# A hybrid transformer block in float32r parts: weight parts and FFN inner tiles at varied byte offsets of SBUF

## The chip, the core and the metric

The kernel runs on one core of a Trainium2 chip. The metric is the time of one execution on the device in microseconds; the median of three runs before the change is 2668.3 us (2667.89 to 2669.66).

## The reference

One sequence of 512 tokens with 1024 features passes a first block and then two equal layers of a second block. All is float32.

```python
def first_block(x, p, ...):                     # once
    z = rms_norm(x, norm1_g) @ w_in             # 1024 -> 2304 columns
    mix = concat(gmlp(z), rglru(z), hgrn2(z), pool(z))
    x = x + mix @ w_out
    hf = causal_dwconv(rms_norm(x, norm2_g) @ w_up, ...)   # 1024 -> 2 x 2816
    gt, val = split(hf)
    x = x + (gelu(gt) * val) @ w_down           # 2816 -> 1024
    gate = sigmoid(rms_norm(x, norm3_g) @ w_pg)
    x = x + (p @ w_pe) * gate
    return rms_norm(x, final_g)

def hybrid_layer(x, ...):                       # twice
    proj = (rms(x) * norm1_g) @ w_in            # 1024 -> 7680
    mixed = g0 * (attention @ w_attn_o) + g1 * (rwkv @ w_rwkv_o) + g2 * (retention @ w_ret_o)
    x = x + mixed @ w_out
    h2 = rms(x) * norm2_g
    return x + (silu(h2 @ w_ffn_gate) * (h2 @ w_ffn_up)) @ w_ffn_down
```

## The kernel before

Activations lie transposed: 128 features on the partitions, 512 tokens along a row, so the model's 1024 features are 8 tiles (k tiles) of 128x512 float32, and the 2816 inner features of an FFN are 22.

**Dense products.** Every product with a weight goes through `mac` (lines 135 to 137). Weight and activation are each split into two float32r parts, high and low, and a product takes three passes: high weight on high activation (line 135), high weight on low activation (line 136), low weight on high activation (line 137). Each pass is a matmul of a 128x128 weight (loaded into the array) on a moving tile of 128x512. An M tile of 128 outputs with 8 k tiles is thus 24 matmuls that add up in one PSUM bank.

**Weights** come in chunks of 8 k tiles (128x1024 float32; 7 k tiles in two of three chunks of the FFNs' second product). `chunk` (line 117) takes a raw chunk that SyncE's queue has loaded (`wraw`, three buffers), lets ScalarE round it into `whi` (line 125) and VectorE subtract that from the raw values into `wlo` (line 126). `whi` and `wlo` have two buffers each, used in turn.

**Activations** are split by `split` (line 172) with the same two engines: `x0h` to `x7l` are the parts of the normed input of a projection, `h0h` to `h21l` the parts of the FFN's inner tiles, `mx` those of the gated sum of the branches, `o` those of attention and retention, `BK` those of the RWKV output (its tiles take the place of keys that are no longer needed), and `t` those of the small input p.

**The FFNs.** `ffn1` (line 655) runs 44 M tiles of w_up on x with a convolution behind each, keeps the 22 products as h tiles, and then runs 8 M tiles of w_down on the 22 h tiles. `ffn2` (line 1342) does the same with gate and up in each of the two layers. In the mixers, dense tiles that nothing waits for are put between the steps of the mixer (`pump`).

**Order.** Instructions are issued in an order that a scheduler makes from the program, and tiles are placed in SBUF by pools in the order in which they are asked for. As built, a row of a partition starts at these bytes, modulo 256:

| tiles | 128x512 matmuls they move in | offset of the moving tile | offset of the weights |
|---|---|---|---|
| x | 6864 | 32 | 32 |
| h | 1584 | 160 | 32 |
| o | 384 | 160 | 32 |
| mx | 384 | 160 | 32 |
| BK | 192 | 0 | 32 |
| t | 48 | 0, 64 or 192 | 32 |

A k tile's weights are 512 bytes of a row, and tiles are 2048 or 4096 bytes long, so the offset is the same for all tiles of a kind, for both buffers and for high and low parts.

Of the kernel before, what the change touches and what calls it, by code (L numbers as in the profile page):

```python
# [11 lines left out]
F32R = mybir.dt.float32r  # L12
# [8 lines left out]
P = 128  # L21
# [13 lines left out]
class Kern:  # L35
    def __init__(self, tc, io, taps=None):
        self.tc, self.nc, self.io = tc, tc.nc, io
        self.taps = taps or {}
        self.n = 0
        self.fill, self.credit = deque(), 0.0  # L40
        self.early = deque()
        self.sx = ""
        self.pa, self.pr, self.pp, self.pi, self.pc, self.pt, self.pl, self.px = 7.0, 4.0, 2.0, 1.7, 2.5, 6.0, 6.0, 5.2

    # Dense tiles that nothing waits for yet are kept in a queue; the mixers let
    # some of them in between their own steps, so that the tensor engine has work.
# [70 lines left out]
    def chunk(self, src):  # L117
        """One chunk of a weight: its float32 values, and their two parts."""
        nc = self.nc
        n = src.shape[-1]  # L120
        raw = self.early.popleft() if self.early else self.fetch(src)
        hi = self.tile(self.wp, [P, 1024], "whi", F32R)
        lo = self.tile(self.wp, [P, 1024], "wlo", F32R)
        with self.tc.high_priority(offset=300):
            nc.scalar.copy(hi[:, :n], raw[:, :n])  # L125
            nc.vector.tensor_tensor(lo[:, :n], raw[:, :n], hi[:, :n].bitcast(F32), ALU.subtract)  # L126
        return hi, lo

    def mac(self, ps, w, xs, first, last):
        """ps += w.T @ x over the k tiles in xs, in three passes."""  # L130
        hi, lo = w
        n = len(xs)
        for k, (xh, xl) in enumerate(xs):
            c = slice(k * P, (k + 1) * P)
            self.nc.tensor.matmul(ps, hi[:, c], xh, start=first and k == 0, stop=False)  # L135
            self.nc.tensor.matmul(ps, hi[:, c], xl, start=False, stop=False)  # L136
            self.nc.tensor.matmul(ps, lo[:, c], xh, start=False, stop=last and k == n - 1)  # L137

    def dense(self, wname, m, xs, kcuts=None):
        """M tile m of a weight applied to the k tiles xs (pairs of parts)."""  # L140
        src = self.io[wname]
        ps = self.tile(self.mm, [P, 512], "mm")
        kcuts = kcuts or [len(xs)]
        k0 = 0
        for i, kn in enumerate(kcuts):
            w = self.chunk(src[m, :, k0 * P:(k0 + kn) * P])
            self.mac(ps, w, xs[k0:k0 + kn], i == 0, i == len(kcuts) - 1)
            k0 += kn
        return ps

    def dense2(self, wname, xs, use):
        """A weight with 4 k tiles: two M tiles to a chunk; use(m, psum)."""
        src = self.io[wname]
        for j in range(src.shape[0]):
            hi, lo = self.chunk(src[j])
            for i in range(2):
                ps = self.tile(self.mm, [P, 512], "mm")
                o = slice(i * 512, (i + 1) * 512)
                self.mac(ps, (hi[:, o], lo[:, o]), xs, True, True)
                use(2 * j + i, ps)  # L160

    def split_into(self, hi, lo, src, scale=1.0):
        """Two float32r parts of src * scale: hi + lo is exact."""
        nc = self.nc
        nc.scalar.activation(hi, src, AF.Copy, scale=scale)  # L165
        if isinstance(scale, float) and scale == 1.0:
            nc.vector.tensor_tensor(lo, src, hi.bitcast(F32), ALU.subtract)
        else:
            nc.vector.scalar_tensor_tensor(lo, src, scale, hi.bitcast(F32), ALU.mult, ALU.subtract)  # L169
        return hi, lo  # L170
# [6 lines left out]
    def rsqrt(self, v, n):  # L177
        """v ** -0.5 for a small [128, n] tile of positive values."""
        nc = self.nc
        y = self.small("rsq", n)  # L180
        t = self.small("rst", n)
        yi = y.bitcast(I32)
        nc.vector.tensor_scalar(yi, v.bitcast(I32), 1, None, ALU.logical_shift_right)
        nc.vector.tensor_scalar(yi, yi, -1.0, float(0x5F3759DF), ALU.mult, ALU.add)
        for _ in range(3):
            nc.vector.tensor_tensor(t, y, y, ALU.mult)
            nc.vector.scalar_tensor_tensor(t, t, -0.5, v, ALU.mult, ALU.mult)
            nc.vector.scalar_tensor_tensor(y, t, 1.5, y, ALU.add, ALU.mult)
        return y

    def bcast(self, col):
        """[128 tokens, 4] -> PSUM [128, 512]: each token's value down a column."""
        ps = self.psum()
        for b in range(NW):
            self.nc.tensor.transpose(ps[:, b * P:(b + 1) * P], col[:, b:b + 1].to_broadcast([P, P]), self.ident)  # L195
        return ps

    def bcast_heads(self, col):
        """[128 tokens, 4 blocks x 2 heads] -> PSUM [2 x 64 features, 512 tokens]."""
# [7 lines left out]
    def token_sum(self, acc, ps, col):  # L207
        """Sum over features of acc into column col + 4 b of ps."""
        for b in range(NW):
            self.nc.tensor.matmul(ps[:, col + b:col + b + 1], acc[:, b * P:(b + 1) * P], self.ones,  # L210
                                  start=True, stop=True)
# [13 lines left out]
    def norm_scale(self, acc):  # L225
        """The broadcast 1 / rms of the tokens, as an SBUF tile."""
# [32 lines left out]
    def mixers1(self, c2, x, xg, rb, pe):  # L259
# [19 lines left out]
        # small parameters  # L279
# [16 lines left out]
        # columns, the longest mixer's first  # L296
# [30 lines left out]
        # p @ w_pe, halved for the gate that comes later  # L327
# [29 lines left out]
        # the order of the k tiles on the host: d, a, b, c  # L357
# [50 lines left out]
    def rglru_consts(self, tp):  # L408
        nc, V = self.nc, self.vec
        # 2 softplus(-lam): e = exp(-|lam|), log1p(e) by the series of atanh  # L410
# [18 lines left out]
        # softplus(-lam) = max(-lam, 0) + 2 acc;  sp = twice that  # L429
# [73 lines left out]
    def hgrn2(self, zq, zf, zig, lvm, tp, yp):  # L503
        nc, V = self.nc, self.vec
        # lower bound: a softmax over the one layer, less its own first row
# [24 lines left out]
        # masked scores [s, t], one level of block size after another  # L530
        # (heads of one parity, a pair of windows: one PSUM bank)
# [57 lines left out]
        # values and decayed keys by token  # L589
# [10 lines left out]
        # states at the starts of the windows, block diagonal over pairs of heads  # L600
# [39 lines left out]
    def head_rms(self, dst, src, nh, tp, xi=None, xi2=None):  # L640
        """dst = src / rms over the last axis of [128, nh, 64] (src in PSUM); of src * xi, where given."""
# [13 lines left out]
    def ffn1(self, x, acc, xg, pe, xs_p):  # L655
        tc, nc, io, V = self.tc, self.nc, self.io, self.vec
        rb = self.norm_scale(acc)
        with tc.tile_pool(name="f1h", bufs=1) as hp, tc.tile_pool(name="f1t", bufs=2) as fp:
            hid = []
            for j in range(FT):  # L660
# [14 lines left out]
                hid.append(self.split(hp, r[1], f"h{j}"))  # L675
# [8 lines left out]
        # the gate, and the two norms that follow it  # L684
# [3 lines left out]
        with tc.tile_pool(name="f1g", bufs=2) as gp:  # L688
# [14 lines left out]
            # y = a / rms(x4) with a = x4 * final_g; with v and w the means of the squares of  # L703
            # x4 and a, the norm of y on top comes to a * (w + EPS * (v + EPS)) ** -0.5
# [42 lines left out]
    def rwkv(self, c):  # L747
# [21 lines left out]
        # halves of parameters that go with tanh  # L769
# [33 lines left out]
        for p in range(4):  # L803
# [3 lines left out]
            # decays  # L807
# [13 lines left out]
            # in-context rate  # L821
# [4 lines left out]
            # keys  # L826
# [13 lines left out]
            # b, scaled; the order of the two halves of a chunk turns with its parity  # L840
# [8 lines left out]
            # bonus  # L849
# [6 lines left out]
            # values by token  # L856
# [6 lines left out]
            # scores  # L863
# [10 lines left out]
            # keys as they stand at the end of the chunk  # L874
# [6 lines left out]
    def rwkv_inverse(self, SC, kp):  # L881
        """The transposed inverses of I - A (64 x 64) in place of the A of SC."""
# [24 lines left out]
        # rows of the first diagonal block, for the block below it  # L907
# [28 lines left out]
    def rwkv_chain(self, SC, AR, BK, UV, end, gd, g2, kp):  # L936
# [29 lines left out]
        def ahead(c):  # L966
            """What a chunk needs apart from the state: decayed keys by token, products with the values."""
# [97 lines left out]
    def evac(self, dst, ps, scale=1.0):  # L1065
        """dst = ps * the tokens' 1 / rms (* scale)."""
# [42 lines left out]
    def att_proj(self, ap):  # L1109
# [10 lines left out]
        # keys and values  # L1120
# [17 lines left out]
        # queries: tile g has head g (of the first key head) over head 4 + g  # L1138
# [66 lines left out]
    def ret_proj(self, rp, rt):  # L1205
        """Queues the columns of the retention, and what is done to them one by one."""
# [48 lines left out]
    def retention(self, rp, op, q, k, vt, sg, cn):  # L1255
        nc, l = self.nc, self.l
        # the queries, keys and values, where the queue still has any
# [61 lines left out]
    def combine(self, oa, oc, mp):  # L1319
        """The gated sum of the three branches (twice it, halved in the split)."""  # L1320
# [21 lines left out]
    def ffn2(self, xd, acc, xg, out):  # L1342
        tc, nc, io, V, l = self.tc, self.nc, self.io, self.vec, self.l
        rb = self.norm_scale(acc)
        with tc.tile_pool(name="f2h", bufs=1) as hp, tc.tile_pool(name="f2t", bufs=2) as fp:
            hid = []
            for j in range(FT):
# [7 lines left out]
                hid.append(self.split(hp, g, f"h{j}"))  # L1355
# [21 lines left out]
def _w(a, per=1, cols=None, rows=None):  # L1377
    """[K, M] -> chunks [M tiles / per, 128, per * K tiles * 128], contiguous for a partition."""
# [13 lines left out]
def _col(v):  # L1392
    """[n * 128] -> [128, n]"""
# [3 lines left out]
def _constants():  # L1397
# [19 lines left out]
    # rotary angles and decays of the retention  # L1417
# [101 lines left out]
```

## Time and profile before

| | |
|---|---|
| median of 3 runs | 2668.3 us |
| span of the profiled execution, first to last instruction | 2666.0 us |
| TensorE matmul busy | 2579.1 us, 97%, 13104 records |
| TensorE weight load busy (beside matmuls) | 2052.8 us, 77% |
| VectorE busy | 1491.5 us, 56% |
| ScalarE busy | 893.7 us, 34% |
| GpSimd busy | 378.5 us, 14% |
| mean granted TensorE clock | 0.985 |

The profile gives for each instruction a start, a duration, its line and its tiles; matmuls are pipelined, so the duration of one reaches beyond the start of the next, and the distance between starts tells how fast they follow each other. [...]

### The profile page before, as it was taken

How to read it: one execution, taken by the hardware profiler on the slowest of the kernel's cores; microseconds unless marked ns; L12 is line 12 of the kernel's file. 1: busy time of each engine (PE TensorE's matmuls, PEld its weight loads, DVE VectorE, ACT ScalarE, POOL GpSimd, SP SyncE). 2: the span in 40 equal slices, each digit the busy share in tenths (PEclk: the TensorE clock that was granted, in tenths of full speed). 3: DMA queues.
4: the chain of work that ended last, by engine and by line, in shares of the span. 5: the costliest groups of instructions: out<-in, count | busy, mean ns of one | idle time of the engine just before them, and what ended most of it. 6: DMA issues, size and time to landing. Idle time of an engine off the chain costs nothing. (4 is left out here: it accounts for less than half of the span.)

```text
span 2666.0 us, 33302 instructions
## 1 busy us (share of the span) xinstructions
PE 2579.1 (97%) x13104; PEld 2052.8 (77%) x13104; DVE 1491.5 (56%) x2546; ACT 893.7 (34%) x1342; POOL 378.5 (14%) x277
## 2 busy tenths in 40 slices
PE   8989999999998999999999999998999999999999
PEld 6767888887776877677788887767877677788887
DVE  8775666336788455565443333788455565444322
ACT  4343444225332333522322222322333423332221
POOL 2111111013120001005311101120000004211100
PEclk9999999999999999999999999999999999999999
DMA  4132223334223143226422334223152226422332
GB/s 148 64 103 85 98 95 95 93 104 139 87 91 107 60 154 95 70 87 206 137 95 97 99 123 127 83 80 107 43 174 88 79 72 213 143 95 95 99 114 96
DMA packets 99502, 282.51 MB, mean 106 GB/s; under 512 B 13201, under 2 KB 14225, under 8 KB 99217
## 3 DMA queue, kind: packets, MB, share of 16 engines
q1 hardware_dynamic: 97616, 277.52, 31.8%
q10 hardware_dynamic: 1728, 2.87, 0.3%
q8 instruction: 103, 1.69, 0.3%
q14 instruction: 55, 0.44, 0.1%
HBM read 244.42 MB, written 31.72 MB: 104 GB/s over the span
## 5 line engine op out<-in xcount | busy, mean ns | idle before, releaser
L125 ACT CAST whi<-wraw 128x1024 fp32r<-128x1024 f32 (+1 forms) x400 | 414.6, 1037 | 1110.1 <-PE mm L136 735.1
L126 DVE TENSOR_TENSOR wlo<-wraw,whi 128x1024 fp32r<-128x1024 f32 (+1 forms) x400 | 491.9, 1230 | 246.6 <-ACT whi L125 237.1
L1352 POOL TENSOR_TENSOR fg<-fg,rb 128x512 f32<-128x512 f32 x44 | 78.3, 1780 | 396.1 <-ACT fg L1351 396.1
L135 PE MATMUL mm<-x0h,whi 128*128 128x512 f32 x286 | 116.2, 407 | 8.1 <-ACT x0h L165 8.1
L220 POOL TENSOR_TENSOR acc<-acc,sq 128x512 f32<-128x512 f32 x49 | 77.8, 1587 | 325.9 <-ACT sq L219 325.9
L137 PE MATMUL mm<-x0h,wlo 128*128 128x512 f32 x286 | 114.1, 399 | 6.0 <-DVE wlo L126 5.7
L135 PE MATMUL mm<-x2h,whi 128*128 128x512 f32 x286 | 114.3, 400 | 2.2 <-ACT x2h L165 2.2
L136 PE MATMUL mm<-x0l,whi 128*128 128x512 f32 x286 | 113.7, 397 | 1.2 <-DVE x0l L169 1.2
L136 PE MATMUL mm<-x2l,whi 128*128 128x512 f32 x286 | 114.6, 401 | 0.0
L136 PE MATMUL mm<-x5l,whi 128*128 128x512 f32 x286 | 112.9, 395 | 1.6 <-DVE x5l L169 1.6
L135 PE MATMUL mm<-x3h,whi 128*128 128x512 f32 x286 | 113.9, 398 | 0.0
L137 PE MATMUL mm<-x1h,wlo 128*128 128x512 f32 x286 | 113.7, 398 | 0.0
L136 PE MATMUL mm<-x3l,whi 128*128 128x512 f32 x286 | 113.1, 395 | 0.7 <-DVE x3l L169 0.7
L137 PE MATMUL mm<-x2h,wlo 128*128 128x512 f32 x286 | 113.7, 398 | 0.0
L136 PE MATMUL mm<-x1l,whi 128*128 128x512 f32 x286 | 113.3, 396 | 0.3 <-DVE x1l L169 0.3
L1354 DVE TENSOR_TENSOR fg<-fg,mm 128x512 f32<-128x512 f32 x44 | 30.3, 688 | 148.8 <-PE mm L137 148.8
L135 PE MATMUL mm<-x5h,whi 128*128 128x512 f32 x286 | 113.4, 397 | 0.0
L137 PE MATMUL mm<-x6h,wlo 128*128 128x512 f32 x286 | 113.3, 396 | 0.0
L135 PE MATMUL mm<-x6h,whi 128*128 128x512 f32 x286 | 113.3, 396 | 0.0
L135 PE MATMUL mm<-x7h,whi 128*128 128x512 f32 x286 | 113.2, 396 | 0.0
L137 PE MATMUL mm<-x7h,wlo 128*128 128x512 f32 x286 | 113.1, 396 | 0.0
L135 PE MATMUL mm<-x1h,whi 128*128 128x512 f32 x286 | 113.1, 395 | 0.0
(757 smaller groups left out, 6132.5 us busy)
## 6 DMA issues: line engine op xcount, KB each, us to landing
wraw<-in_w_in_dram SPq DMA_DIRECT2D x138, 512.0 KB, 3.5
wraw<-in_w_ffn_dram SPq DMA_DIRECT2D x88, 512.0 KB, 3.4
wraw<-in_w_up_dram SPq DMA_DIRECT2D x44, 512.0 KB, 3.3
wraw<-in_w_ffn_down_dram SPq DMA_DIRECT2D x32, 448.0 KB, 3.4
wraw<-in_w_out_dram SPq DMA_DIRECT2D x24, 512.0 KB, 3.5
gates<-gt SPq DMA_DIRECT2D x48, 256.0 KB, 2.1
cg<-gates SPq DMA_DIRECT2D x32, 256.0 KB, 3.8
gt<-xres SPq DMA_DIRECT2D x32, 256.0 KB, 3.3
```

The costliest lines, as they stand in the source:

```text
L125: nc.scalar.copy(hi[:, :n], raw[:, :n])
L126: nc.vector.tensor_tensor(lo[:, :n], raw[:, :n], hi[:, :n].bitcast(F32), ALU.subtract)
L135: self.nc.tensor.matmul(ps, hi[:, c], xh, start=first and k == 0, stop=False)
L136: self.nc.tensor.matmul(ps, hi[:, c], xl, start=False, stop=False)
L137: self.nc.tensor.matmul(ps, lo[:, c], xh, start=False, stop=last and k == n - 1)
L220: (eng or nc.gpsimd).tensor_tensor(acc, acc, s, ALU.add)
L1352: nc.gpsimd.tensor_tensor(g, g, rb, ALU.mult)
L1354: nc.vector.tensor_tensor(g, g, ps, ALU.mult)
```

## The change

No instruction is added, removed or moved: on each of the five engines the instructions, their order and their waits are the same. What changes is where two kinds of tiles start in SBUF.

```diff
     def chunk(self, src):
         raw = self.early.popleft() if self.early else self.fetch(src)
-        hi = self.tile(self.wp, [P, 1024], "whi", F32R)
-        lo = self.tile(self.wp, [P, 1024], "wlo", F32R)
+        o = 8 * (self.nw % 4)
+        self.nw += 1
+        hi = self.tile(self.wp, [P, 1056], "whi", F32R)[:, o:o + 1024]
+        lo = self.tile(self.wp, [P, 1056], "wlo", F32R)[:, o:o + 1024]
...
+    def split_at(self, pool, src, tag, o):
+
+        hi, lo = (self.tile(pool, [P, T + 8], tag + c, F32R)[:, o:o + T] for c in "hl")
+        return self.split_into(hi, lo, src)
...
     # ffn1
-                hid.append(self.split(hp, r[1], f"h{j}"))
+                hid.append(self.split_at(hp, r[1], f"h{j}", 0))
...
     # ffn2
-                hid.append(self.split(hp, g, f"h{j}"))
+                hid.append(self.split_at(hp, g, f"h{j}", 2 + 2 * l))
```

The rest of the diff takes out comments. The tiles of `whi` and `wlo` are 128 bytes longer, so the two buffers start 128 apart modulo 256, and a chunk's parts start another 0, 32, 64 or 96 bytes in, by the chunk's number modulo 4. The h tiles are 32 bytes longer, so each next one (h0h, h0l, h1h, ...) starts 32 bytes further on modulo 256; in the two layers of the second block they start another 8 and 16 bytes in. As built:

| tiles | offset before | offset after |
|---|---|---|
| whi, wlo | 32 | 32, 192, 96, 0, chunk by chunk |
| h in ffn1 | 160 | 160, 192, 224, 0, 32, 64, 96, 128 in turn |
| h in ffn2 of the first layer | 160 | the same and 8 |
| h in ffn2 of the second layer | 160 | the same and 16 |
| x, o, mx, BK, t | as above | unchanged |

## Rows read from the trace of the kernel before

**Rows 1.** The page: span, and busy time with share and count.
```profile
span 2666.0 us, 33302 instructions
PE 2579.1 (97%) x13104; PEld 2052.8 (77%) x13104; DVE 1491.5 (56%) x2546; ACT 893.7 (34%) x1342; POOL 378.5 (14%) x277
```
**Rows 2.** Stretch, length; busy us (count) of PE, PEld, DVE, ACT, POOL; clock; DMA.
```profile
250.00:460.00 210.00, 210.00 (x929) 173.87 (x927) 140.56 (x212) 93.30 (x117) 25.14 (x20) 1.00 0.29 97
480.00:580.00 100.00, 100.00 (x431) 80.41 (x430) 31.09 (x33) 26.54 (x32) 7.76 (x5) 1.00 0.31 92
640.00:950.00 310.00, 284.81 (x1950) 224.48 (x1949) 225.94 (x426) 105.97 (x161) 40.85 (x32) 0.96 0.27 92
```
**Rows 3.** Timeline of TensorE, w_up of ffn1: start us, duration us, operation.
```profile
399.70 0.39 PE L135 MATMUL mm<-x3h,whi 128*128 128x512 f32 x1
...
401.97 0.39 PE L136 MATMUL mm<-x6l,whi 128*128 128x512 f32 x1
```
**Rows 4.** Timeline of TensorE, w_up at a granted clock of 0.50, and that clock.
```profile
234.81 0.63 PE L136 MATMUL mm<-x4l,whi 128*128 128x512 f32 x1
...
238.23 0.63 PE L135 MATMUL mm<-x7h,whi 128*128 128x512 f32 x1
...
235.00:239.00 4.00, 4.00 (x11) 0.50 0.00 0
```
**Rows 5.** Timeline of TensorE, w_down of ffn1.
```profile
474.06 0.39 PE L136 MATMUL mm<-h0l,whi 128*128 128x512 f32 x1
474.28 0.40 PE L137 MATMUL mm<-h0h,wlo 128*128 128x512 f32 x1
474.75 0.40 PE L136 MATMUL mm<-h1l,whi 128*128 128x512 f32 x1
...
476.39 0.39 PE L137 MATMUL mm<-h3h,wlo 128*128 128x512 f32 x1
```
**Rows 6.** Timeline of TensorE, output projection of the first layer.
```profile
1265.69 0.40 PE L136 MATMUL mm<-mx4l,whi 128*128 128x512 f32 x1
...
1268.94 0.40 PE L135 MATMUL mm<-mx1h,whi 128*128 128x512 f32 x1
```
**Rows 7.** Timeline of TensorE, RWKV output projection of the first layer.
```profile
951.10 0.40 PE L135 MATMUL mm<-BK,whi 128*128 128x512 f32 x1
...
952.97 0.40 PE L136 MATMUL mm<-BK,whi 128*128 128x512 f32 x1
```
**Rows 8.** Timeline of TensorE, projection tiles after a break in attention.
```profile
1089.10 0.40 PE L137 MATMUL mm<-x5h,wlo 128*128 128x512 f32 x1
...
1091.41 0.39 PE L135 MATMUL mm<-x1h,whi 128*128 128x512 f32 x1
```
**Rows 9.** Groups by line of TensorE: count, busy us, mean ns, idle before.
```profile
L135 PE MATMUL mm<-x3h,whi 128*128 128x512 f32 x286 | 113.9, 398 | 0.0
L135 PE MATMUL mm<-h0h,whi 128*128 128x512 f32 x24 | 9.5, 398 | 0.0
L136 PE MATMUL mm<-o,whi 128*128 128x512 f32 x128 | 50.5, 394 | 0.0
L136 PE MATMUL mm<-BK,whi 128*128 128x512 f32 x64 | 25.5, 399 | 0.0
L135 PE MATMUL mm<-mx2h,whi 128*128 128x512 f32 x16 | 6.3, 395 | 0.0
L135 PE MATMUL mm<-t,whi 128*128 128x512 f32 x16 | 6.5, 405 | 0.0
```
**Rows 10.** Groups by line of VectorE: count, busy us, mean ns, idle before.
```profile
L671 DVE SCALAR_TENSOR_TENSOR fc<-fe,pv,fc 128x512 f32<-128x512 f32 x88 | 65.9, 749 | 2.5 <-ACT fc L669 0.9
L1350 DVE TENSOR_TENSOR fg<-mm,rb 128x512 f32<-128x512 f32 x44 | 30.4, 692 | 114.0 <-PE mm L137 113.8
L667 DVE TENSOR_TENSOR fe<-mm,rb 128x512 f32<-128x512 f32 x44 | 30.3, 688 | 24.2 <-PE mm L137 24.2
L850 DVE SCALAR_TENSOR_TENSOR t<-t,pv,t 128x512 f32<-128x512 f32 x8 | 5.9, 740 | 0.0
```

More of the change, by code (lines that the diff above doesn't have):

```diff
@@ L39, in __init__ @@
         self.n = 0
+        self.nw = 0
         self.fill, self.credit = deque(), 0.0
```

## The prediction

> **What bounds the kernel now.** I read the busy shares first: TensorE is busy 2579.1 of the 2666.0 us of the span, 97%, and no other engine comes near it [rows 1]. So I asked next where it does not stand still at all. In the rows by stretch it is busy for the whole of 250 to 460 us (tiles of w_up, moving tiles x) and of 480 to 580 us (tiles of w_down, moving tiles h), at a granted clock of 1.00; in the mixers, 640 to 950 us, it is busy 284.81 of 310 us [rows 2]. In an FFN the time is thus a number of matmuls times the distance from one start to the next, and that distance is the only thing that moving data in SBUF can change. The order and the waits of all five engines are the same in both programs.
>
> The distance is read from starts in the timeline. Moving tiles x, at byte 32 of 256 as the weights are: ten starts from 399.70 to 401.97, 0.227 us each [rows 3]. [...] Moving tiles h, at byte 160 with weights at 32: ten starts from 474.06 to 476.39, 0.233 us each, alternately 0.22 to 0.23 and 0.23 to 0.24 [rows 5]. Tiles mx, also 160 against 32: 14 starts in 3.25 us, 0.2321 [rows 6]. Tiles BK, 0 against 32: eight in 1.87 us, 0.2338 [rows 7]. Same shape, same engine, same clock: what differs is where the moving tile lies. After a break x needs some ten starts to come back to its pace: 2.31 us for ten from 1089.10 on, 0.231 each [rows 8].
>
> So of the three pairs of offsets that can be seen for long, two run at 0.232 to 0.234, and one, equal offsets, at 0.2267, the value I use for it: it lies between the 0.227 of the starts and the 0.226 of the 929 matmuls in 210 us, those cut at the ends counted [rows 2].
>
> **The change part by part.** The counts: 24 groups of 286 matmuls on x (6864), 66 groups of 24 on h (1584), and 3 times 128 on o, 3 times 64 on BK, 24 times 16 on mx, 48 on t (1008) [rows 9]. 3168 of the 6864 are in the three FFNs (44 M tiles of 24 matmuls each, three times); 3696 are in projections.
>
> 1. *Weights at 32, 192, 96 and 0 in turn, x still at 32.* A quarter of the chunks keeps the equal pair, three quarters get pairs that the trace does not show. Bounds for such a pair: 0.2267, if it settles as the equal pair does, and 0.2338, the slowest seen. One of three pairs seen settles, so I take two of the new ones at 0.233 and one at the value of a pair that settles. A chunk has 24 matmuls and now differs from the chunk ahead, so even a pair that settles must first find its pace: ten at 0.231 and 14 at 0.2267 are 0.2285 on the average. The three new pairs then give (2 x 0.233 + 0.2285)/3 = 0.2315, and with the quarter at 0.2285 the mean is 0.2308. In the FFNs: 3168 x (0.2308 - 0.2267) = +13.0 us, with nothing beside it, since TensorE never stops there. In the projections there are breaks already, so I start from 0.2275: 3696 x 0.0033 = +12 us. Of this part the mixers hide some, where TensorE waits for others for 25 of 310 us [rows 2]; but what waits there waits for VectorE and ScalarE chains that in their turn wait for matmuls behind the dense tiles, so I count three quarters, +9 us.
>
> 2. *h tiles 32 bytes further apart, and 0, 8 or 16 bytes on by FFN.* The moving offset now changes from one matmul to the next and runs through eight values against four of the weights; 1584 matmuls. No settled pattern can form. Bounds 0.2267 and 0.2338 again; I take 0.232, between the 0.231 of unsettled x and the 0.233 of h today: 1584 x -0.0013 = -2 us.
>
> 3. *o, mx, BK, t against the varied weights.* 1008 matmuls at 0.232 to 0.234 today, and I leave them there: 0, and at the bounds -6 or +1 us.
>
> 4. *ScalarE and VectorE read and write the same tiles at odd offsets.* The trace has this already: the multiply that writes 8 bytes into its tile takes 688 ns, the one that writes from the tile's start 692; the multiply-add that reads 4 and 8 bytes in takes 749, one that reads from the start 740 [rows 10]. 0 us; even 9 ns on each of the 800 splits of weights would lie on engines that are busy 56% and 34% of the span [rows 1].
>
> 5. *More SBUF* (512 bytes a partition for weights, 32 a tile of h): no instruction and no wait changes. 0.
>
> [...]
>
> Sum: 13.0 + 9 - 2 = +20 us. The profiled execution has a span of 2666.0 us and the median of the runs is 2668.3, so 2.3 us lie around the span: 2666.0 + 20 + 2.3 = 2688 us.
>
> **The rivals.**
>
> *Nothing settles (slower still).* Each chunk breaks the pace and no new pair settles: x runs at 0.2325 throughout. 3168 x 0.0058 + 3696 x 0.005 x 0.75 - 2 = 18.4 + 13.9 - 2 = +30, 2698 us; at 0.2338 for all x it would be +40. For it: two of three pairs seen. Against it: the equal pair stays in a quarter of the chunks.
>
> *Only the moving tile's own offset counts (no change).* x stays at 32 and at 0.2267 whatever the weights do; h takes a mean over eight offsets, say 0.230: 1584 x -0.0033 = -5, 2663 us, and about 2668 if h stays. For it: in the trace the weights never move, so the two causes cannot be told apart. [...]
>
> *Spreading works (faster).* Weights and moving data that start in different places stay out of each other's way; x keeps 0.2267 and h, mx, o and BK come down to it: -1584 x 0.0066 - 1008 x 0.006 = -16.5, 2652 us. It decides if unequal offsets cost less than equal ones. [...] Against it: the only equal pair in the trace is the fastest one. [...]
>
> **How the numbers follow.** Forecast (one or two of the new pairs settle) 0.42; nothing settles 0.23; only the moving tile counts 0.18; spreading works 0.17. The likeliest gives 2688 us. Its own range is 2678 (all three new pairs settle within their chunk, +10) to 2696. The range to hold the time 8 times in 10 leaves out most of the gain below and the slowest pace for all x above: 2658 to 2703. What a measurement of this kernel can tell from no change is about 0.2%, 5.3 us. Slower: the first two cases nearly whole, 0.64. No change: most of the third and the edges of the first, 0.16. Faster: the fourth and the end of the third where h gains its 5 us, 0.20.
>
> **What would show it.** In the profile after, starts in the w_up stretch should be 0.227 us apart in at most a quarter of the chunks and 0.23 or more in the others, and 1000 matmuls there should take some 231 us instead of 227. In w_down the even alternation should be gone and the mean be near 0.232. Durations on ScalarE and VectorE should stay. The forecast is wrong if x stays at 0.227 in chunks of all four weight offsets (third case), if any chunk runs steadily below 0.2267 (fourth), or if the mixers take the slower tiles without getting longer.

## The result, and the profile after

| | us | runs |
|---|---|---|
| before, median | 2668.1 | 4 (2667.68 to 2669.66) |
| after, median | 2686.44 | 4 (2681.3 to 2686.72) |
| after / before | 1.0065 | 95% interval 1.005 to 1.0079 |
| span of the profiled execution, before | 2666.0 | |
| span of the profiled execution, after | 2684.9 | |

The changed kernel is slower by 18.3 us, 0.65%. The forecast was 2688 us. The page of the changed kernel (span, then busy time, share of the span and count of each engine) shows where it lies:

```profile
span 2684.9 us, 33302 instructions
PE 2602.1 (97%) x13104; PEld 2052.2 (76%) x13104; DVE 1490.5 (56%) x2546; ACT 894.0 (33%) x1342; POOL 378.7 (14%) x277
```

Against [rows 1], matmul busy time has grown by 23.0 us with the same 13104 matmuls, while VectorE, ScalarE and GpSimd differ by at most 1 us: all of it is on TensorE. The windows of the changed kernel in w_up and w_down (stretch, length, busy us and count of PE, PEld, DVE, ACT, POOL, clock, DMA share, GB/s) answer to the first two of [rows 2]:

```profile
250.00:460.00 210.00, 210.00 (x907) 170.06 (x907) 137.47 (x208) 90.17 (x115) 24.56 (x19) 1.00 0.30 96
480.00:590.00 110.00, 110.00 (x476) 89.05 (x475) 36.00 (x39) 30.75 (x37) 9.03 (x6) 1.00 0.33 97
```

In w_up the same 210 us, at the same clock and without a gap, hold 907 matmuls in place of 929. In w_down 476 fit into 110 us, 0.231 each, and before 431 into 100, 0.232 each: no loss there. In the mixers the same stretch of time no longer holds the same work; they are read further down, between equal places of the program.

Where x lost is plain from the first matmul of each chunk of 24. The timeline of TensorE in the changed kernel (start us, duration us, operation), w_up of ffn1, five chunks, whose weights lie at byte 32, 192, 96, 0 and 32 again:

```profile
304.12 0.39 PE L138 MATMUL mm<-x0h,whi 128*128 128x512 f32 x1
...
309.57 0.39 PE L138 MATMUL mm<-x0h,whi 128*128 128x512 f32 x1
...
315.17 0.39 PE L138 MATMUL mm<-x0h,whi 128*128 128x512 f32 x1
...
320.77 0.40 PE L138 MATMUL mm<-x0h,whi 128*128 128x512 f32 x1
...
326.37 0.39 PE L138 MATMUL mm<-x0h,whi 128*128 128x512 f32 x1
```

The chunk at 32, where x lies too, takes 5.45 us, 0.2271 a matmul; the other three take 5.60 us each, 0.2333. Duration says nothing of this, 0.39 or 0.40 us throughout: only the starts do. Over the whole trace, at full clock and without breaks, the distance between starts of x within a chunk is 0.2276 with weights at 32, 0.2335 at 192, 0.2332 at 96 and 0.2332 at 0.

In w_down the order of one slow and one less slow start [rows 5] is gone. TensorE's timeline of the changed kernel, the first nine products of w_down:

```profile
482.10 0.40 PE L138 MATMUL mm<-h0h,whi 128*128 128x512 f32 x1
482.33 0.40 PE L139 MATMUL mm<-h0l,whi 128*128 128x512 f32 x1
482.56 0.39 PE L140 MATMUL mm<-h0h,wlo 128*128 128x512 f32 x1
482.80 0.39 PE L138 MATMUL mm<-h1h,whi 128*128 128x512 f32 x1
...
484.18 0.39 PE L138 MATMUL mm<-h3h,whi 128*128 128x512 f32 x1
```

Nine in 2.08 us are 0.231; the mean over all h is 0.2322, before 0.2333.

A budget of the whole program follows from the first matmul of each stretch. The timelines give these starts for ffn1 and the stretch behind it, first of before:

```profile
227.04 0.39 PE L135 MATMUL mm<-x0h,whi 128*128 128x512 f32 x1
...
473.82 0.40 PE L135 MATMUL mm<-h0h,whi 128*128 128x512 f32 x1
...
597.02 0.39 PE L135 MATMUL mm<-x0h,whi 128*128 128x512 f32 x1
```

and of after:

```profile
230.15 0.39 PE L138 MATMUL mm<-x0h,whi 128*128 128x512 f32 x1
...
482.10 0.40 PE L138 MATMUL mm<-h0h,whi 128*128 128x512 f32 x1
...
604.58 0.39 PE L138 MATMUL mm<-x0h,whi 128*128 128x512 f32 x1
```

w_up went from 473.82 - 227.04 = 246.78 to 251.95 us (+5.2), w_down from 123.20 to 122.48 (-0.7), and the next 350 us, with gate, projections and the RWKV mixer up to its output at 948.29 and 955.18, from 351.27 to 350.60 (-0.7). Read so throughout, from the first matmul to the last:

| stretch | after minus before, us |
|---|---|
| projections and mixers of the first block | +3.0 |
| w_up; gate and up of the two layers | +5.2, +6.6, +5.3 |
| w_down; down of the two layers | -0.7, -0.1, -0.9 |
| last gate and projections up to the RWKV output, twice | -0.7, -0.7 |
| RWKV output to attention output, twice | +1.0, +1.0 |
| the output projections of attention, retention and the layer (o, mx) | -0.2 |
| sum | +18.8 |

The +6.6 holds about 1.3 us of clock: the windows from 1298 us of the changed kernel and from 1290 us of the kernel before, the same place (stretch, length, PE busy and count, granted clock):

```profile
1298.00:1310.00 12.00, 10.74 (x46) 0.86 0.35 109
```
```profile
1290.00:1302.00 12.00, 10.60 (x53) 1.00 0.34 115
```

A stretch of 3.4 us at a granted clock of 0.50 (half clock) stands in the one trace and not in the other, though TensorE is idle for 1.3 to 1.4 of the 12 us in both; nothing in the runs ties it to the offsets. The stretches of the mixers hold differences of clock too, which e5 and e6 bring out.

### The profile page after: what moved, and what is told of

The parts are those of the page before. It is cut to its first block, busy times and chain, and to the rows that moved or that the text cites. A ratio compares the mean times of both kernels' runs of the same rounds, so it can differ in the third digit from the quotient of the medians.

```text
span 2684.9 us, 33302 instructions
## 1 busy us (share of the span) xinstructions
PE 2602.1 (97%) x13104; PEld 2052.2 (76%) x13104; DVE 1490.5 (56%) x2546; ACT 894.0 (33%) x1342; POOL 378.7 (14%) x277
## 5 line engine op out<-in xcount | busy, mean ns | idle before, releaser
L128 ACT CAST whi<-wraw 128x1024 fp32r<-128x1024 f32 (+1 forms) x400 | 414.0, 1035 | 1132.0 <-PE mm L139 756.7
L129 DVE TENSOR_TENSOR wlo<-wraw,whi 128x1024 fp32r<-128x1024 f32 (+1 forms) x400 | 491.2, 1228 | 241.0 <-ACT whi L128 231.8
L139 PE MATMUL mm<-x7l,whi 128*128 128x512 f32 x286 | 114.4, 400 | 0.0
L140 PE MATMUL mm<-x5h,wlo 128*128 128x512 f32 x286 | 114.1, 399 | 0.0
```

## The experiments

Five questions were open: whether the weights' offsets or the h tiles' do it; whether the difference of moving tile and weights counts or a byte of its own; whether it is the variation; how much the mixers hide; and whether the width of the weight load sets the distance. The quoted expectations number the theories. All times are medians; ratios stand against the kernel before on the same chip and are not quotients of the medians.

| run | us | ratio (95%) |
|---|---|---|
| e1: only the weights varied | 2684.2 | 1.0057 (1.0044 to 1.0071) |
| e2: weights moved to the tiles' offset | 2657.27 | 0.9957 (0.9945 to 0.997) |
| e3: tiles moved to the weights' offset | 2656.86 | 0.9954 (0.994 to 0.9967) |
| e4: weights in steps of 4 bytes | 2682.64 | one run |
| e5: weights varied in the FFNs alone | 2680.48 | 1.0039 (1.0026 to 1.0052) |
| e6: weights varied in projections alone | 2672.53 | 1.001 (1.0 to 1.0019) |
| e7: difference 112 throughout | 2687.89 | 1.0072 (1.0057 to 1.0087) |
| e8: difference 228 throughout | 2688.79 | 1.007 (1.0049 to 1.0091) |
| e9: weight loads of 64 columns | 2662.24 | one run |
| e10: weight loads of 32 columns | 2675.07 | one run |

**e1, the weights alone.** The chunk's part of the change, h tiles as before:

```diff
+        o = 8 * (self.nw % 4)
+        self.nw += 1
+        hi = self.tile(self.wp, [P, 1056], "whi", F32R)[:, o:o + 1024]
+        lo = self.tile(self.wp, [P, 1056], "wlo", F32R)[:, o:o + 1024]
```

> Only the weights at 32, 192, 96 and 0 in turn; h tiles stay at 160. Theory 1 (the pace hangs on the difference of moving and weight offset modulo 256, and only a difference of zero settles at 0.2267 us; h matters little): x as in the changed kernel, 0.2279 us with weights at 32 and 0.233 with the others; h near 0.2325; time 2687 us, within 2 us of the changed kernel. Theory 2 (most of the loss comes from the h tiles that start 8 or 16 bytes off, and x only loses by the change of offset from chunk to chunk): w_down gets back to 0.233, the time falls below 2680 us.

The time, 2684.2 us, can't be told from the changed kernel's 2686.44. PE's windows of e1 (as above, PE alone):

```profile
250.00:460.00 210.00, 210.00 (x908) 1.00 0.29 95
490.00:590.00 100.00, 100.00 (x432) 1.00 0.33 96
```

x has 908 matmuls in 210 us as in the changed kernel (907), 0.2320 from starts, and w_down is 0.6 us shorter in each FFN although its tiles stay where they were. So the loss comes from the weights' offsets against x, and the h tiles' own spread is worth no more than a microsecond. Theory 1 holds here, its rival falls.

**e2 and e3, equal offsets from either side.** e2 gives a chunk the offset of the tiles it will meet, 32 floats (128 bytes) on for h, mx and o, 56 floats for BK; e3 leaves the weights alone and moves the tiles by a pad of 128 bytes:

```diff
     # e2
-    def chunk(self, src):
+    def chunk(self, src, o=0):
...
+        hi = self.tile(self.wp, [P, 1088], "whi", F32R)[:, o:o + 1024]
+        lo = self.tile(self.wp, [P, 1088], "wlo", F32R)[:, o:o + 1024]
...
-                ps = self.dense("w_down", m, hid, [8, 7, 7])
+                ps = self.dense("w_down", m, hid, [8, 7, 7], 32)
...
     # e3
+        nc.vector.memset(self.tile(self.tiny, [P, 32], "pad", bufs=1), 0.0)
```

> The weights of each product start at the offset of its moving tiles: 32 for x, 160 for h, o and mx, 0 for BK. The tiles themselves stay. Theory 1 (difference): h, o, mx and BK come down from 0.232 to 0.234 to 0.2267, -10.5 us for 1584 matmuls on h, -4 for 768 on o and mx, -1 for 192 on BK: 2653 us. Theory 3 (byte 32 itself is the good place for a moving tile, whatever the weights do): h stays at 0.233, 2668 us. Theory 4 (offsets matter through the change from chunk to chunk): x unchanged, h at 0.2267 or 0.233 alike.

> One unused tile of 128 bytes ahead of the later pools puts h, o and mx at 32, where the weights are; BK goes from 0 to 128 against 32. Theory 1: h, o, mx at 0.2267, BK unchanged near 0.233: 2654 us. Theory 3 (byte 32 is the good place): the same 2654 us, so this run and the one with moved weights tell theories 1 and 3 apart only together. If both are at 2668, neither holds and the difference between x and h is of another kind.

Both are faster than before, by 11 us. TensorE's timeline in w_down of ffn1, e2 and then e3:

```profile
475.73 0.39 PE L136 MATMUL mm<-h0l,whi 128*128 128x512 f32 x1
...
478.00 0.39 PE L137 MATMUL mm<-h3h,wlo 128*128 128x512 f32 x1
```
```profile
475.87 0.39 PE L137 MATMUL mm<-h0l,whi 128*128 128x512 f32 x1
...
478.14 0.39 PE L138 MATMUL mm<-h3h,wlo 128*128 128x512 f32 x1
```

Ten starts take 2.27 us in both, and 2.33 before [rows 5]: 0.2267 in all three FFNs. In e2 h, mx and o lie at 160 with their weights at 160, in e3 both at 32, and the pace is the same; so in these two it is the difference that counts and no byte of its own. mx and o come to 0.2275 and 0.2273 in e2, 0.2269 to 0.2271 in e3; BK to 0.2278 in e2, where its weights follow it, and it stays at 0.2338 in e3, where it lies at 128 against 32. The starts give what was expected: in e2 3.5 us in each FFN, 10.5 in all, and 4.8 on o, mx and BK. That the time fell by 11 us and not by 15 is in part the clock: in the profiled execution of e2, 8.4 us shorter by the span, half clock cost 6.2 us more than in that of before. e2's five executions were granted 0.984 on the mean, nine of the kernel before 0.985. PE's windows of e2 for x, untouched, and for h:

```profile
250.00:460.00 210.00, 210.00 (x928) 1.00 0.30 98
485.00:585.00 100.00, 100.00 (x443) 1.00 0.33 101
```

x as before (929 in [rows 2]), h 443 in 100 us in place of 431: h went from 0.2333 to 0.2267 by moving weights alone.

**e4, many differences.** The weights move on by 4 bytes every six chunks:

```diff
+        o = (self.nw // 6) % 64
+        self.nw += 1
+        hi = self.tile(self.wp, [P, 1088], "whi", F32R)[:, o:o + 1024]
```

> Weights advance by 4 bytes every six chunks, 64 offsets in all, so that one profile shows the pace of about 144 matmuls at each difference. Theory 1 in its plain form: 0.2267 us at a difference of 0 alone, 0.231 to 0.234 elsewhere, with something near 0.229 at 64 (o and mx with weights at 96 in the changed kernel). A wider form: a band of some bytes around 0 is as good, and there may be differences that run below 0.2267. Time between 2680 and 2700 us.

Mean distance of starts at full clock by the difference, moving tile less weights modulo 256:

```
difference   72    76    80    120   124   128   132   136   224   228   232
x (us)     .2324 .2334 .2301 .2333 .2270 .2334 .2316 .2278 .2333 .2350 .2311
h (us)     .2320 .2333 .2301 .2333 .2270 .2334 .2316 .2272 .2333 .2350 .2311
```

x and h agree, kind of tile and place in the program apart, which is what theory 1 asks. PE's windows of e4: x at 128, x at 124, h at 128, h at 124:

```profile
1346.00:1376.00 30.00, 30.00 (x130) 1.00 0.28 91
1380.00:1409.00 29.00, 29.00 (x130) 1.00 0.32 93
2597.00:2625.00 28.00, 28.00 (x121) 1.00 0.41 126
2628.00:2655.00 27.00, 27.00 (x121) 1.00 0.42 130
```

130 matmuls in 30 us at 128 and in 29 us at 124, 121 in 28 and in 27 us: 4 bytes decide. Equal offsets are not the only fast ones: x at 28 and at 112 stands at 0.2267 too. No difference ran settled below 0.2267, so none of those tried has more to give than the equal pair. Small steps do not help as such: x at a difference of 8 stands at 0.2333.

**e5 and e6, FFNs and projections apart.** The changed kernel's weights in the one, in the other its two buffers' bytes without the chunk's step (offsets 32 and 32):

```diff
+        o = 8 * (self.nw % 4) if self.vary else 32 * (self.nw % 2)
...
     # e5; e6 has "not (...)"
+        self.vary = (wname == "w_up" or wname == "w_down" or "ffn" in wname)
```

> The weights take the four offsets in turn in the three FFNs alone; everywhere else they stay at 32 as before. If the projections' slower tiles are hidden by the mixers (theory A, from the stretches of the changed kernel, where they grew by 3.6 us in all), nearly the whole loss is here: +17 for w_up and gate/up, -2 for w_down, 2683 us. If my forecast of the projections holds (theory B: +9 on the path), this run keeps only some 11 of 18 us: 2679 us.

> The reverse: weights at four offsets in turn in all products outside the FFNs, at 32 in the FFNs. 3696 matmuls on x slow down by some 4 to 5 ns each, 17 us of matmul distance. Theory A (hidden by the mixers): 2668 to 2672 us. Theory B (three quarters on the path): 2677 to 2681 us.

PE's windows of e5, then of e6:

```profile
250.00:460.00 210.00, 210.00 (x907) 1.00 0.28 95
```
```profile
250.00:460.00 210.00, 210.00 (x928) 1.00 0.30 98
```

e5's FFN stretches are longer by 5.36, 5.34 and 5.33 us in w_up and its likes and shorter by 0.62 in each down product: +14.2 us net. In e6 w_up is as before (929 in [rows 2]), so the longer weight tiles and the second buffer's other place cost nothing by themselves. The times do not decide between the theories. e6 costs 2.7 us by the ratio, 0 to 5 within the interval, and 3.9 by the medians, which is near theory A; e5 costs 10.4 and 11.9, which is nearer theory B.

What blurs them is the granted clock, which differs from one execution to the next, 0.985 to 0.988 in e5's five and 0.984 to 0.988 in e6's ten. TensorE's windows from the end of the first layer's FFN to the second layer's RWKV output, the same matmuls each time: before, e2, e5 and the changed kernel:

```profile
1656.37:1955.13 298.76, 278.75 (x1917) 0.95 0.26 88
```
```profile
1649.77:1953.34 303.57, 283.40 (x1918) 0.93 0.26 87
```
```profile
1664.21:1959.28 295.07, 273.97 (x1917) 0.97 0.27 90
```
```profile
1670.64:1968.66 298.02, 278.19 (x1917) 0.97 0.27 89
```

In the first three x has its equal pair there, and yet the stretch takes 298.76, 303.57 and 295.07 us, shorter the higher the clock. The changed kernel's 298.02 us are 0.7 less than before, but 3.0 more than e5's, also at 0.97. The other such stretch, from the gate to the first layer's RWKV output, before, changed and e6:

```profile
597.02:948.29 351.27, 325.49 (x2133) 0.97 0.30 99
```
```profile
604.58:955.18 350.60, 327.11 (x2134) 0.97 0.30 99
```
```profile
599.87:951.65 351.78, 328.80 (x2134) 0.96 0.30 99
```

TensorE stands idle there (length less busy) for 25.8, 23.5 and 23.0 us: idle time gives back 2 to 3 us. As the matmuls have one order in all these kernels, each distance between starts can be set against the same one before. Outside the FFNs the distances of x at full clock and without a break grow by 13.4 us in sum, in the changed kernel and in e6 alike; the distances at breaks and of the mixers' own matmuls shrink by 6.4 and 6.7. So about half of the slower pace is hidden and some 7 us are left on the path. In the changed kernel the share differs by stretch: 2.9 of 3.7 us are hidden up to the first layer's RWKV output, 1.1 of 2.7 up to the second layer's, and 0.3 of 2.5 in the first block. Places where one of the two traces is at half clock add -3.2 us in the changed kernel and +0.6 in e6. Neither theory holds as it stands: far less is hidden than A says, and three quarters on the path was too much. Whether the offsets themselves raise the clock, 0.986 to 0.989 in the changed kernel's executions and 0.984 to 0.986 in 14 of the kernel before, is not shown.

**e7 and e8, other constant differences.** e2's parameter with other numbers, 36/4/28 floats for a difference of 112 and 7/39/63 for 228, the same for all chunks that meet one kind of tile:

```diff
-    def chunk(self, src):
+    def chunk(self, src, o=36):      # e8: o=7
...
+                ps = self.dense("w_down", m, hid, [8, 7, 7], 4)      # e8: 39
```

> Every product has its weights 112 bytes below its moving tiles (176 for x, 48 for h, o and mx, 144 for BK): no offset is equal. Theory 1 in the form that the probe left (only the difference counts; 0, 28, 112 and 124 settle at 0.2267): as fast as with equal offsets, 2657 us. Plain theory 1 (equality alone): x near 0.233, 2690 us.

> The control: weights 228 bytes below the moving tiles everywhere, the slowest difference of the probe that ran steadily on both x and h (0.235). Theory 1: x in the FFNs 3168 x 0.0083 = +26 us, h 1584 x 0.0017 = +2.7, projections hidden but for some 4: 2700 us, slower than the changed kernel although nothing varies. If variation itself were the cause (theory 4), a constant offset runs as before, 2668 us.

PE's windows of e7: x of w_up, h of ffn1, x and h of the first layer's FFN; then the same of e8:

```profile
260.00:460.00 200.00, 200.00 (x859) 1.00 0.29 95
490.00:600.00 110.00, 110.00 (x473) 1.00 0.32 97
1320.00:1540.00 220.00, 220.00 (x944) 1.00 0.28 93
1560.00:1660.00 100.00, 100.00 (x443) 1.00 0.42 132
```
```profile
260.00:460.00 200.00, 200.00 (x852) 1.00 0.28 93
490.00:600.00 110.00, 110.00 (x473) 1.00 0.32 93
1320.00:1540.00 220.00, 220.00 (x938) 1.00 0.29 94
1560.00:1660.00 100.00, 100.00 (x443) 1.00 0.41 128
```

In neither does an offset vary from chunk to chunk, and both are as slow as the changed kernel (2687.89 and 2688.79 us against 2686.44): variation is not what costs here. But theory 1 in the form "each difference has its pace" falls too. e4 had x at 0.2267 at 112; in e7 x runs at 0.2333 throughout, and h, at the same 112, at 0.2333 in ffn1 (473 in 110 us) and at 0.2267 in the layers (443 in 100 us). In e8, at 228, h runs at 0.2333 in ffn1, 0.2267 in the first layer and 0.2333 in the second, and x at 0.2350 in ffn1 and the first layer and at 0.2334 in the second; 2700 us were expected and 2688.79 came. One difference thus ran settled at more than one pace. What chooses between them is not shown. Zero is the one difference that came to 0.2267 in every FFN stretch in which it stayed the same throughout.

**e9 and e10, narrower weight loads.** If x and h run at two paces because the weight load and the moving tile get in each other's way, which no run shows, a load of fewer columns should shorten the distance. These leave out the outputs behind the first 64 (e10: 32) columns in all but the first and last matmul of a product:

```diff
-            self.nc.tensor.matmul(ps, hi[:, c], xl, start=False, stop=False)
+            g = slice(k * P, k * P + 64)      # e10: 32
+            self.nc.tensor.matmul(ps[:64], hi[:, g], xl, start=False, stop=False)
```

> Offsets as before, but all matmuls of a product except the first and the last load only 64 of their 128 weight columns, so half of each dense output leaves out most of its terms. [...]

> The same with 32 weight columns. [...]

The weight load's rows (shortest/median/longest ns), before, e9 and e10:

```profile
L136 PEld LDWEIGHTS mm<-x0l,whi x286: 186/188/330, 9.9 to 2533.5; 128*128 128x128 f32 x143
```
```profile
L138 PEld LDWEIGHTS mm<-x0l,whi x286: 132/134/223, 9.8 to 2529.9; 128*64 128x64 f32 x143
```
```profile
L138 PEld LDWEIGHTS mm<-x0l,whi x286: 106/108/174, 10.1 to 2542.1; 128*32 128x32 f32 x143
```

PE's windows of w_up and w_down, e9 and then e10:

```profile
260.00:460.00 200.00, 200.00 (x872) 1.00 0.29 95
480.00:580.00 100.00, 100.00 (x438) 1.00 0.33 97
```
```profile
260.00:460.00 200.00, 200.00 (x867) 1.00 0.29 95
485.00:585.00 100.00, 100.00 (x436) 1.00 0.32 93
```

The load went from 188 to 134 to 108 ns, but by its starts the distance of x in w_up, the equal pair, rose from 0.2267 to 0.2298 and 0.2311, and that of h fell from 0.2333 to 0.2294 and 0.2306. The distance neither shrinks with the load, since that of x rose, nor stays. That the two get in each other's way is thus not shown, and where the two paces come from stays open.

## Why the prediction was right, and where its steps were not

The time was right, 2688 against 2686.4, and so were the cause (unequal offsets cost, by the weights' part of the change) and the sign. The sum +20 came out at +18.8 by stretches, but its two largest terms were off, by +4.1 and -5.4 us: that the sum is so near is in part luck.

*Only the distance between starts changes.* Right: the splits of the weights on ScalarE and VectorE took 1035 and 1228 ns on the average, before 1037 and 1230. Terms 4 and 5, at zero, hold; in the three down products h tiles another 0, 8 and 16 bytes in gave -0.7, -0.1 and -0.9 us, where e1 with unmoved tiles gave -0.6 each.

*Term 1, FFNs: forecast +13.0, measured +17.1 in the profile, 16.0 in e5's, which lacks the stretch of half clock in the first layer.* The step that failed is "one of three pairs seen settles, so I take two of the new ones at 0.233 and one at the value of a pair that settles". None came down to 0.2267: 0.2332 to 0.2335 for all three. A count of three is no rate; that the only equal pair was the one that ran fast would have been the better reading of the same rows. The quarter that keeps its pair found its pace sooner than I took (0.2271 in the chunk read above, against 0.2285). Together x came to 0.2320, not 0.2308. On this step the first rival, with 0.2325, was nearer than the forecast.

*Term 1, projections: forecast +9, measured +3.6 (e6: 2.7, between 0 and 5).* The slower pace itself was sized about right, 13.4 us against 12. "I count three quarters" was too high, and it made the first rival's 2698 too high as well. I argued that what waits in the mixers hangs on matmuls behind the dense tiles; that holds for about half of it, some 7 us, and the other half went into shorter breaks. The rest of the distance down to 3.6 is clock: the changed kernel's trace stood less at half clock in the mixers, worth 3.2 us, which no term of the sum had and no run ties to the offsets. By that the last sign of being wrong, mixers that take the slower tiles without getting longer, came up in the stretches up to the RWKV output (-0.7 each) and not in the others (+3.0, +1.0, +1.0).

*Term 2, h: forecast -2, measured -1.7.* Right in size, and the alternation is gone. But e1 has about the same (-0.6 an FFN) with the h tiles where they were: varying the weights alone gave as much.

*Term 3, o, mx, BK: forecast 0, measured -0.2 for o and mx and -0.4 for BK from its starts (0.2337 to 0.2317).*

*The range.* The lower end of the likeliest case, +10 with all three new pairs settled within their chunk, is not what its own terms give: 3168 x 0.0018 + 3696 x 0.001 x 0.75 - 2 is +6.5. The result lies far from it.

*The rivals.* That only the moving tile's offset counts is refuted by x, which never moved (0.2276 with weights at 32, 0.2332 to 0.2335 with the others). Spreading as a gain is refuted by e1, e4 and e8 (2684.2, 2682.64 and 2688.79 us), the gain being where offsets are equal (e2 and e3, 2657.27 and 2656.86).

## What to carry to other kernels

When matmuls of one shape follow each other without a gap, read the distance of their starts for each kind of moving tile apart: two paces at one clock are a difference worth finding, though here durations (0.39 or 0.40 us) and the busy share (97% before and after) didn't show it. Here the moving tile and the weights, both float32r, should start at the same byte modulo 256 (half of that is not enough: x at a difference of 128 ran at 0.2334 in e4; whether a longer period counts was not tried): one pad of 128 bytes (e3) or weights placed to fit (e2) took the kernel from 2668 to 2657 us, ahead of both versions, while the spread cost 18. And a cost that lands in a stretch with breaks can be hidden in part: here about half was paid, some 7 of 13.4 us, and what is left is read between equal places of two traces at the same granted clock: in the mixers one stretch took 295 to 304 us with the same offsets of x at a clock of 0.97 to 0.93.

## What the runs showed of the hardware

- At a granted clock of 1.00 the two commonest settled paces of matmuls of 512 columns were 0.2267 and 0.2333 us; e8's x at 0.2350 is a third. At 0.50 eight starts of x took 3.42 us, 0.4275 each [rows 4], less than twice the 0.2267 (0.4533). Unequal offsets cost nothing there: x in the changed kernel stands at 0.427 at half clock with weights at 32, 96 and 192 alike (41, 14 and 7 distances).
- At one difference (112) both paces were seen, for as long as an FFN's product lasts, in one program (h in e7, 473 matmuls in 110 us and 443 in 100).
- The pace changed with 4 bytes of offset: 0.2333 at 120, 0.2270 at 124, 0.2334 at 128 (e4).
- The distance did not shrink in step with the weight load: at 134 ns and 108 ns a load, equal pairs ran at 0.2298 and 0.2311 and unequal ones at 0.2294 and 0.2306 (e9, e10), and at 188 ns at 0.2267 and 0.2333.
